# A hymba-style layer on one core: TensorE's order in the input stages written out by hand, with five queues of small steps behind the projection matmuls

## The chip, the core and the metric

The kernel runs on one core of a Trainium2 chip. A core has TensorE (PE in the profile, with its weight loads as PEld), VectorE (DVE), ScalarE (ACT), GpSimd (POOL), SyncE (SP, which issues the DMAs here) and 16 DMA engines. The metric is the device time of one execution in microseconds. Of the kernel before, three timed runs gave 1741.38 to 1743.57 us, with a median of 1742.06 us.

## The reference, cut to what matters

One transformer layer is applied to a prompt of 1024 tokens and to a sample sequence of 64 tokens (with a cache of 256 past frames and a recurrent state). All arrays are float32.

```python
def _layer(x, c, shift_prev, s_prev, k_past, v_past, logf_past, ...):
    mod = jax.nn.silu(c) @ w_ada + b_ada
    sh1, sc1, gt1, sh2, sc2, gt2 = jnp.split(mod, 6, axis=-1)
    h = _rms_norm(x, norm1_g) * (1 + sc1[:, None]) + sh1[:, None]
    proj = h @ w_in
    p_rwkv, p_fox = proj[..., :RWKV_COLS], proj[..., RWKV_COLS:]
    prev = jnp.concatenate([shift_prev, p_rwkv[:, :-1]], axis=1)
    z = p_rwkv + (prev - p_rwkv) * shift_mu
    r, k, v, dw, da, dg = jnp.split(z, list(RWKV_SPLITS), axis=-1)
    w_log = -jax.nn.softplus(-(w0 + jnp.tanh(dw) @ w_decay_up)) - 0.5
    decay = jnp.exp(-jnp.exp(w_log))
    a = jax.nn.sigmoid(a0 + da @ w_aaa_up)
    g = jax.nn.sigmoid(dg) @ w_gate_up
    kk = _heads(k * k_k, RWKV_HEADS)
    kk = kk / jnp.maximum(jnp.linalg.norm(kk, axis=-1, keepdims=True), 1e-12)
    k = k * (1 + (a - 1) * k_a)
    y, s_new = _rwkv_scan(r, decay, k, v, kk, a, s_prev)   # per token: S = S*w + (S.-kk)(kk*a)' + v k'
    y = group_norm(y) * gn_g + gn_b
    y_rwkv = (y + bonus(r, k, r_k, v)) * g
    q, kf, vf, fl = jnp.split(p_fox, list(FOX_SPLITS), axis=-1)
    q, kf = _rms_norm(q, fox_q_g), _rms_norm(kf, fox_k_g)
    logf = jax.nn.log_sigmoid(fl + fox_f_b)
    y_fox = _fox_mixer(q, k_all, v_all, cumsum(logf_all), past)   # causal softmax with a decay bias
    x = x + gt1[:, None] * (jnp.concatenate([y_rwkv, y_fox], axis=-1) @ w_out)
    h2 = _rms_norm(x, norm2_g) * (1 + sc2[:, None]) + sh2[:, None]
    x = x + gt2[:, None] * ((silu(h2 @ w_ffn_gate) * (h2 @ w_ffn_up)) @ w_ffn_down)
    return x, s_new, ...
```

The width is 1024, there are 8 rwkv heads and 8 attention ("fox") heads of 64, and the inner width of the last block is 2816.

## The kernel before, in words

Activations lie transposed, features on partitions. The tokens come in two halves (`Half`): the first has 512 tokens of the prompt and is one chunk of 512 columns; the second has the other 512 and the 64 sample tokens, in two chunks of 288. A float32 product is made of three fp32r matmuls, high by high, high by low and low by high, so that a projection column (128 outputs) takes 8 x 3 matmuls for each chunk (`mm3`, L294 to L296, tile `pmm`).

The kernel runs through a start (modulation, first norm), the input stage of the first half, that of the second half, the attention of both halves with the output product between, and the gated block with its down product. The change touches the two input stages alone, that is `phase` and what it calls. Each has 26 projection columns: two for the low-rank inputs (12 and 13), three for each of four pairs of rwkv heads (letter Z, in `proj_z`), and four each of Q, K and V for the attention. "Head" below stands for such a pair of rwkv heads. Around the columns stand these pieces, each with matmuls that are small:

- D, `rwkv_d` (L388): decay and learning rate of a head, from a low-rank product.
- A, `rwkv_a` (L417): key norm (`bsum`, L375), the chunk matrices pA (L464, 64*128 shapes), their masked copy `At`, a trip of 16x16 blocks through DRAM, and a solve of 31 small operations on VectorE (L485 to L491).
- B, `rwkv_b` (L500): the rest of the inversion in five groups of 32x32 matmuls (L523 and L549), transposes (L567, L575), and the state chain. It goes chunk by chunk (8 in the first half, 9 in the second): pR (L597), its copy R by VectorE and ScalarE (L599, L600), pSA (L610), its negated copy sv (L611, L612), pS (L613), and the new state (L617), with two pY beside it.
- N, `rwkv_n` (L628): group norm and gate of a head. L, `logf`: forget gates. q and k, `fox_norm` (L763): the norm of a Q or K column. C, `cache_kv`: cached keys and values. S, `x_stat1`: the norm of the second half's input. The modulation steps of the later stages (`ada_mm`, `ada_fin`) come from a list called `background`, one in front of each column.

`ORDER` gives the order in which these pieces are traced, as whole pieces, by letter and head. The order in which the engines run them is not this one. The framework's scheduler keeps a list of instructions for each engine, and picks by place in the trace and by its own estimate of when operands are ready, so that a later projection matmul may go ahead of an earlier small one. The order that it picks is then fixed in the program, and each engine runs its own in order. In the second half, the state chain of the last head (its B and N, `late`) is traced behind the input stage, and overlaps with the first half's attention.

PSUM has 8 banks: two for `mm` (projection, modulation, forget gates, statistics), two for `ra`, one for `fx`, one for `rb`, two for `ch`. Weights come through a ring of four raw tiles `wraw` (also used for modulation and for statistics), and are split into high (ScalarE, L212) and low (VectorE, L216). SP issues all DMAs.

Of the kernel before, what the change touches and what calls it, by code (L numbers as in the profile page):

```python
# [7 lines left out]
F32 = mybir.dt.float32  # L8
# [26 lines left out]
ORDER = ("Z0 D0 A0 L B0 D1 Z1 Q0 N0 A1 C0 Z2 q0 D2 V0 O A2 K0 k0 B1 K1 Z3 Q1 q1 V1 N1 D3 A3 V2 C1 S k1 Q2 Q3 B2 q2 N2 K2 k2 V3 K3 k3 C2 C3 q3",  # L35
         "T3 Z0 D0 A0 L Z1 K0 D1 U3 B0 A1 D2 Z2 Q0 N0 k0 A2 q0 D3 Q1 B1 K1 q1 Z3 A3 k1 V2 N1 V1 B2 V0 Q2 q2 K3 N2 Q3 q3 P B3 K2 k3 k2 V3")
# [28 lines left out]
class K:  # L65
# [115 lines left out]
    def ada_mm(self, t, raw=None, ptag="mm"):  # L181

        nc = self.nc
        if raw is None:
            raw = self.ada_load(t)
        ps = self.ps([P, 2, P], tag=ptag, name="pada")
        for s in range(2):
            for i in range(4):
                k = 2 * i + s
                last = nc.tensor.matmul(ps[32 * i:32 * i + 32, 0], self.ct[:, k], raw[:, k], start=(s == 0),  # L190
                                        stop=(s == 1))
        row = self.slot([P, P], name="mrow", tag="mrow")
        return t, ps, row, last, nc.scalar.copy(row, ps[:, 0])

    def ada_fin(self, part):
        nc = self.nc
        t, ps, row = part[:3]
        self.last = nc.tensor.transpose(ps[:, 1], row, self.ident)
# [33 lines left out]
    def x_stat1(self):  # L232

        nc = self.nc
        acc = self.zpool.tile([P, 576], F32, tag="z", name="xacc")
# [12 lines left out]
        return self.x_rms(Half(1), acc)  # L248

    def x_rms(self, hf, rs):  # L250
        nc, n = self.nc, hf.n
        for off, m in hf.chunks:
            ps = self.ps([P, 512], tag="mm", name="pxs")
            nc.tensor.matmul(ps[:, 0:m], self.ones, rs[:, off:off + m], start=True, stop=True)
            nc.scalar.activation(rs[:, off:off + m], ps[:, 0:m], AF.Ln, scale=1.0 / D, bias=self.eps_n)
# [53 lines left out]

    def proj_z(self, hf, zi):  # L310
# [8 lines left out]
        z = self.zpool.tile([P, 576], F32, tag="z", name="z")  # L319
# [44 lines left out]
    def lora(self, hf, j, w, rows, x, evac, tag):  # L364
        nc = self.nc
        for off, n in hf.chunks:
            ps = self.ps([P, 512], tag=tag, name="plora")
            nc.tensor.matmul(ps[:, 0:n], w[rows, j * P:(j + 1) * P], x[rows, off:off + n], start=True, stop=True)
            evac(ps[:, 0:n], off, n)

    def bsum(self, hf, w, x, evac, tag):
        nc = self.nc
        for off, n in hf.chunks:
            ps = self.ps([P, 512], tag=tag, name="pbs")
            nc.tensor.matmul(ps[:, 0:n], w, x[:, off:off + n], start=True, stop=True)  # L375
# [12 lines left out]
    def rwkv_d(self, hf, j, zl):  # L388
# [6 lines left out]
        for off, m in hf.chunks:  # L395

            ps = [self.ps([P, 512], tag="ra", name="plora") for _ in range(2)]
            for x in range(2):
                nc.tensor.matmul(ps[x][:, 0:m], self.whi2[x][:, j * P:(j + 1) * P], zl[:, x, off:off + m], start=True,
                                 stop=False)  # L400
            for x in range(2):
                nc.tensor.matmul(ps[x][:, 0:m], self.wlo2[x][:, j * P:(j + 1) * P], zl[:, x, off:off + m], start=False,
                                 stop=True)
            for x, (dst, base) in enumerate(((sw, V_W0), (a, V_A0))):
                nc.vector.tensor_scalar(dst[:, off:off + m], ps[x][:, 0:m], col(base), -43.0, op0=ALU.add, op1=ALU.max)
        self.sigm(sw[:, 0:n], 1.0)
        self.sigm(a[:, 0:n], 1.0)
        cum = self.slot(name="cum", tag="sa")
# [6 lines left out]
        return a, cum  # L415

    def rwkv_a(self, hf, j, z, d):  # L417

        nc, vc, O = self.nc, self.vc, self.O
# [4 lines left out]
        zk, zr, zv, sq = z  # L424
        a, ip = d
        pp = self.pp
# [5 lines left out]
            rn[:, off:off + m], ps, 1e-24, None, op0=ALU.max), "ra")  # L432
        nc.scalar.activation(rn[:, 0:n], rn[:, 0:n], AF.Ln, scale=1.0 / 64)
        nc.scalar.activation(rn[:, 0:n], rn[:, 0:n], AF.Exp, scale=-0.5)
        kk = self.slot(name="kk", tag="sa")
        nc.vector.scalar_tensor_tensor(kk[:, 0:n], zk[:, 0:n], self.kk8[:, j:j + 1], rn[:, 0:n], op0=ALU.mult, op1=ALU.mult)
        rk = self.rpool.tile([P, 9, P], F32, tag="rk", name="rk")
        kb = self.rpool.tile([P, 9, P], F32, tag="kb", name="kb")
        nc.vector.tensor_tensor(rk[:, 0:nch, 0:64], ch(kk), pp[:, 0:nch, 0:64], op=ALU.mult)
        nc.vector.tensor_tensor(rk[:, 0:nch, 64:128], ch(zr), pp[:, 0:nch, 1:65], op=ALU.mult)  # L440
        nc.vector.tensor_tensor(kk[:, 0:n], kk[:, 0:n], a[:, 0:n], op=ALU.mult)
        for h in range(2):
            hp = slice(64 * h, 64 * h + 64)
            nc.vector.tensor_tensor(kb[hp, 0:nch, hp], ch(kk)[hp], ch(ip)[hp], op=ALU.mult)
        nc.vector.tensor_scalar(a[:, 0:n], a[:, 0:n], col(V_KA), self.oka[:, j:j + 1], op0=ALU.mult, op1=ALU.add)
        nc.vector.tensor_tensor(zk[:, 0:n], zk[:, 0:n], a[:, 0:n], op=ALU.mult)
        for h in range(2):
            hp, oc = slice(64 * h, 64 * h + 64), slice(64 - 64 * h, 128 - 64 * h)
            nc.vector.tensor_tensor(kb[hp, 0:nch, oc], ch(zk)[hp], ch(ip)[hp], op=ALU.mult)

        nc.vector.scalar_tensor_tensor(zr[:, 0:n], zr[:, 0:n], col(V_RK), zk[:, 0:n], op0=ALU.mult, op1=ALU.mult)
        bon = self.slot(name="bon", tag="bon")
        self.bsum(hf, self.bones, zr, lambda ps, off, m: nc.vector.tensor_tensor(
            bon[:, off:off + m], ps, zv[:, off:off + m], op=ALU.mult), "ra")

        At = self.rpool.tile([P, 9, 2, 2, 64], F32, tag="At", name="At")
        for c in range(0, nch, 4):
# [3 lines left out]
            for i in range(m):  # L461
                for h in range(2):
                    hp = slice(64 * h, 64 * h + 64)
                    nc.tensor.matmul(pa[h][:, i], kb[hp, c + i], rk[hp, c + i], start=True, stop=True)  # L464
            for h in range(2):
                nc.vector.tensor_tensor(At[:, c:c + m, :, h], pa[h][:, 0:m].rearrange("p i (x t) -> p i x t", x=2),
                                        self.amask[:, h:h + 1].rearrange("p o (x t) -> p o x t", x=2)
                                        .to_broadcast([P, m, 2, 64]), op=ALU.mult)

# [9 lines left out]
        nc.sync.dma_start(mb[0:2 * nb], dm.rearrange("i g x s t -> (i g x) s t"))  # L479
        wb = self.rpool.tile([72, 16, 16], F32, tag="wb", name="wb")  # L480
# [4 lines left out]
        for s in range(15):  # L485
# [4 lines left out]
            nc.vector.tensor_tensor(wb[0:2 * nb, s + 1:16, 0:s + 1], wb[0:2 * nb, s + 1:16, 0:s + 1], t_, op=ALU.add)  # L490
        nc.vector.tensor_copy(mb[0:2 * nb], wb[0:2 * nb].rearrange("p s t -> p t s"))  # L491
# [6 lines left out]
        return zv, rk, kb, pc, bon, At, dw, du  # L498

    def rwkv_b(self, hf, j, st):  # L500

        zv, rk, kb, pc, bon, At, dw, du = st
        nc, vc, O = self.nc, self.vc, self.O
        n, nch = hf.n, hf.nch
        ng = 2 * nch
        col = lambda base: vc[:, base + j:base + j + 1]

# [7 lines left out]

        def small(name, blocks, mm):

            pg = [self.ps([P, 9, 32], tag=t, name=name) for t in ("rb", "ch")]
            for c in range(nch):
                for x in blocks:  # L520
                    for h in range(2):
                        r = slice(64 * h + 32 * x, 64 * h + 32 * x + 32)
                        nc.tensor.matmul(pg[h][r, c], *mm(h, c, r, slice(32 * x, 32 * x + 32)), start=True, stop=True)  # L523
# [4 lines left out]
        for h in range(2):  # L528
            hs = slice(64 * h, 64 * h + 64)
            nc.vector.tensor_tensor(g1[hs, 0:nch], pg[h][hs, 0:nch],  # L530
                                    self.qmask[hs].unsqueeze(1).to_broadcast([64, nch, 32]), op=ALU.mult)
        pg = small("pw1", (0,), lambda h, c, r, o: (inv[r, c, r], g1[r, c]))
        for h in range(2):
            r = slice(64 * h, 64 * h + 32)
            nc.vector.tensor_tensor(gt[r, 0:nch, 0:16], gt[r, 0:nch, 0:16], pg[h][r, 0:nch, 0:16], op=ALU.add)
        pg = small("pu1", (0, 1), lambda h, c, r, o: (g1[r, c], inv[r, c, r]))
# [1165 lines left out]
```

## Time and profile before

| | us |
|---|---|
| timed runs, median (lowest to highest) | 1742.06 (1741.38 to 1743.57) |
| the profiled execution, its own time | 1735.94 |
| its span, first to last instruction | 1734.2 |
| PE busy in the span | 1663.8 |
| VectorE busy | 1126.6 |
| ScalarE busy | 729.1 |
| first column of the first half's input stage starts | 35.0 |
| first column of the second half's starts | 329.8 |
| last projection matmul of the second half starts | 692.2 |

A row of a group reads: line, engine, operation, out<-in by the program's names, shape, count | busy us, mean ns of one | idle time of the engine before it, and what ended most of it. A row of a stretch reads: the stretch, its length, then the busy us (and instruction count) of PE, PEld, DVE, ACT and POOL, then the clock granted to TensorE as a share of the full one, the mean busy share of the DMA engines, and GB/s. A row of the timeline reads: start, duration, engine, line, operation, out<-in, shape, count. A float32 matmul that is not of the fp32r kind shows as two records. The ends of matmuls are modelled, so that the distance from one start to the next tells more than the duration. A row of waits reads: engine and line, the engine and line that released it, us in total, times, longest.

### The profile page before, as it was taken

To read this page: it belongs to the slowest core of one execution; us is meant where nothing else is said; L and a number is where in the kernel's file an instruction comes from. 1 tells how busy PE (TensorE), PEld (TensorE's weight loads), DVE (VectorE), ACT (ScalarE), POOL (GpSimd) and SP (SyncE) were. 2 spreads that over 40 slices of the span, in tenths; PEclk is the share of its full clock that TensorE was granted. 3 is DMA by queue.
4 is the path that set the end of the run, shared out by engine and by line. 5 is a ranking of instruction groups with operands and counts; after the bars stand their busy time and mean duration, and the time that the engine had idled before them with its cause. 6 is when DMAs were issued, how large, how long until landed. Compare 5 with 4: busy or idle time off the path is not lost.

```text
span 1734.2 us, 33257 instructions
## 1 busy us (share of the span) xinstructions
PE 1663.8 (96%) x12893; PEld 1447.9 (83%) x12893; DVE 1126.6 (65%) x2574; ACT 729.1 (42%) x1532; POOL 180.8 (10%) x412
## 2 busy tenths in 40 slices
PE   5999999999999999889999989999999999999999
PEld 3676766688888888766888889999999999999998
DVE  6676676757686753876877686666666655555545
ACT  4534454553454445765776453333233223211210
POOL 2102121131221212300210000000000000000000
PEclk9999999999899999989999999999999999999999
DMA  8535457632233344566553333222222224433213
GB/s 314 149 95 137 142 140 207 175 93 56 55 76 75 95 121 136 157 194 177 151 177 136 127 115 101 75 75 75 76 75 82 78 87 143 161 98 98 95 37 122
DMA packets 133581, 207.09 MB, mean 119 GB/s; under 512 B 62126, under 2 KB 70350, under 8 KB 133422
## 3 DMA queue, kind: packets, MB, share of 16 engines
q1 hardware_dynamic: 133422, 204.95, 39.3%
q8 instruction: 102, 1.67, 0.4%
q14 instruction: 57, 0.47, 0.1%
HBM read 157.65 MB, written 47.25 MB: 118 GB/s over the span
## 4 chain that ended last, share of the span: by engine, by line
PE 82%; DVE 7%; ACT 7%; DMA 2%; issue 2%; SPq 1%; POOL 0%; DVEq 0%; ACTq 0%; POOLq 0%
PE pd L1264 15%; PE pfc L1153 8%; PE pfe L1153 8%; PE pfa L1153 7%; PE pmm L294 5%; PE pmm L296 5%; PE pmm L295 5%; PE pfb L1153 4%; PE pav L962 2%; PE pbs L375 2%; PE pA L464 2%; PE ppt L940 2%; PE po L294 1%; PE po L295 1%; PE po L296 1%
## 5 line engine op out<-in xcount | busy, mean ns | idle before, releaser
L294 PE MATMUL pmm<-hhi,whi 128*128 128x288 f32 (+1 forms) x624 | 220.7, 354 | 0.7 <-ACT pb L317 0.7
L295 PE MATMUL pmm<-hlo,whi 128*128 128x288 f32 (+1 forms) x624 | 218.2, 350 | 0.0
L296 PE MATMUL pmm<-hhi,wlo 128*128 128x288 f32 (+1 forms) x624 | 218.0, 349 | 0.0
L212 ACT CAST whi<-wraw 128x1024 fp32r<-128x1024 f32 (+2 forms) x116 | 99.3, 856 | 214.4 <-PE pd L1264 167.0
L1264 PE MATMUL pd<-ah,wlo 128*128 128x512 f32 (+1 forms) x528 | 173.5, 329 | 0.0
L1264 PE MATMUL pd<-al,whi 128*128 128x512 f32 (+1 forms) x528 | 173.2, 328 | 0.0
L1264 PE MATMUL pd<-ah,whi 128*128 128x512 f32 (+1 forms) x528 | 173.0, 328 | 0.0
L1268 DVE SCALAR_TENSOR_TENSOR x1t<-pd,mod,x1t 128x512 f32<-128x512 f32 x192 | 91.4, 498 | 110.6 <-PE pd L1264 110.0
L294 PEld LDWEIGHTS pmm<-hhi,whi 128*128 128x128 f32 x624 | 120.3, 193 | 13.5 <-ACT pb L317 2.0
L296 PEld LDWEIGHTS pmm<-hhi,wlo 128*128 128x128 f32 x624 | 120.3, 193 | 10.9 <-issue 1.7
L295 PEld LDWEIGHTS pmm<-hlo,whi 128*128 128x128 f32 x624 | 120.4, 193 | 9.6 <-issue 0.7
L216 DVE TENSOR_TENSOR wlo<-wraw,whi 128x1024 fp32r<-128x1024 f32 (+2 forms) x108 | 103.8, 961 | 26.0 <-ACT whi L212 25.6
L1153 PE MATMUL pfc<-hh,hS 128*128 128x256 f32 (+1 forms) x352 | 102.0, 290 | 4.4 <-ACT hh L1055 4.4
L1264 PEld LDWEIGHTS pd<-al,whi 128*128 128x128 f32 x528 | 99.4, 188 | 7.7
L1264 PEld LDWEIGHTS pd<-ah,whi 128*128 128x128 f32 x528 | 99.3, 188 | 7.7
L1264 PEld LDWEIGHTS pd<-ah,wlo 128*128 128x128 f32 x528 | 99.2, 188 | 7.4
L1153 PE MATMUL pfc<-hl,hS 128*128 128x256 f32 (+1 forms) x352 | 102.3, 290 | 0.0
L1153 PE MATMUL pfc<-hh,lS 128*128 128x256 f32 (+1 forms) x352 | 102.0, 290 | 0.0
L1153 PE MATMUL pfa<-hl,whi 128*128 128x256 f32 (+1 forms) x352 | 101.8, 289 | 0.0
L1153 PE MATMUL pfa<-hh,whi 128*128 128x256 f32 (+1 forms) x352 | 101.7, 289 | 0.0
L1153 PE MATMUL pfa<-hh,wlo 128*128 128x256 f32 (+1 forms) x352 | 101.4, 289 | 0.0
L604 POOL TENSOR_SCALAR sd<-sv,pc 64x64 f32<-64x64 f32 x136 | 72.0, 529 | 172.9 <-DVE sv L617 156.6
(360 smaller groups left out, 4402.0 us busy)
## 6 DMA issues: line engine op xcount, KB each, us to landing
wraw<-in_w_in_dram SPq DMA_DIRECT2D x52, 512.0 KB
wada<-in_w_ada_dram SPq DMA_DIRECT2D x48, 512.0 KB
as<-actscr SPq DMA_DIRECT2D x22, 544.0 KB
wraw<-in_w_gate_dram SPq DMA_DIRECT2D x22, 512.0 KB
wraw<-in_w_up_dram SPq DMA_DIRECT2D x22, 512.0 KB
wraw<-in_w_down_dram SPq DMA_DIRECT2D x40, 256.0 KB
wraw<-in_w_out_dram SPq DMA_DIRECT2D x16, 512.0 KB
actscr<-sg SPq DMA_DIRECT2D x22, 288.0 KB
```

Of the source, the lines that this page charges most:

```text
L212: nc.scalar.copy(hi, src)
L216: eng.tensor_tensor(lo, src, hi.bitcast(F32), op=ALU.subtract)
L294: nc.tensor.matmul(ps[0:M, 0:n], whi[:, k, 0:M], xhi[:, k, off:off + n], start=(k == 0), stop=False)
L295: nc.tensor.matmul(ps[0:M, 0:n], whi[:, k, 0:M], xlo[:, k, off:off + n], start=False, stop=False)
L296: nc.tensor.matmul(ps[0:M, 0:n], wlo[:, k, 0:M], xhi[:, k, off:off + n], start=False, stop=(k == kt - 1))
L375: nc.tensor.matmul(ps[:, 0:n], w, x[:, off:off + n], start=True, stop=True)
L464: nc.tensor.matmul(pa[h][:, i], kb[hp, c + i], rk[hp, c + i], start=True, stop=True)
L604: nc.gpsimd.tensor_scalar(sd[hsl[h]], sv[hsl[h], c, h], pc[hsl[h], c], None, op0=ALU.mult)
L940: nc.tensor.transpose(pt[0:rows, b - b0, t * P:t * P + qn], p[0:qn, pc:pc + rows], self.ident[0:qn, 0:qn])
L1153: nc.tensor.matmul(ps, l[:, k], r[:, s, k], start=(first and k == 0 and y == 0), stop=(k == 3 and y == 2), skip_group_check=True)
L1264: nc.tensor.matmul(ps[:, 0:n], w[:, i], x[:, t:t + n], start=(i == 0 and y == 0), stop=(i == len(fs) - 1 and y == 2))
L1268: nc.vector.scalar_tensor_tensor(dst, ps[:, so - off:so - off + l], self.mod[:, 40 + o, b:b + 1], dst, op0=ALU.mult, op1=ALU.add)
```

## The change

All matmuls and transposes of the two input stages, from the column after the low-rank ones on, are pinned in the order in which they are traced: `self.te` is a wrapper, `Ordered`, that ties each PE instruction to the one traced before it. Other engines and the DMA queue are left to the scheduler, and so is PE in all other stages.

The pieces become generators, which give way between their steps. Five queues (`Jobs`) hold them: B the state chains, X the pieces D and A, Y the inversions (now a piece of their own, `rwkv_m`), F modulation, forget gates, fox norms, values and cache, and G norms and statistics. After every three projection matmuls `proj` calls `tick`, which takes one step from some of the queues: in the first half from B, X, Y and, in turn, F or G; in the second half in turn from B and X or from Y, F and G. `pause` lets a number of ticks pass, `drain` steps the queues with no projection between until a condition holds.

Other edits come with it. The raw weights are asked for two columns ahead, by a `plan` (`next_raw`), and split in the column before. `ORDER` is shorter, since B, N, q and k are now queued by their producers. P, which loads the first attention operands, waits until the last head's solve has been traced. The last head's chain and norm end in the input stage, and `late` is gone. `ch` has one bank in place of two, a new `yb` has one (the inversion and the transposes; both halves of a group share it), modulation and forget gates move from `mm` to `fx`, norms from `rb` to `ra`, and the slots `sb` are three in place of two.

```diff
-ORDER = ("Z0 D0 A0 L B0 D1 Z1 Q0 N0 A1 C0 Z2 q0 D2 V0 O A2 K0 k0 B1 K1 Z3 Q1 q1 V1 N1 D3 A3 V2 C1 S k1 Q2 Q3 B2 q2 N2 K2 k2 V3 K3 k3 C2 C3 q3",
-         "T3 Z0 D0 A0 L Z1 K0 D1 U3 B0 A1 D2 Z2 Q0 N0 k0 A2 q0 D3 Q1 B1 K1 q1 Z3 A3 k1 V2 N1 V1 B2 V0 Q2 q2 K3 N2 Q3 q3 P B3 K2 k3 k2 V3")
+ORDER = ("L O D0 Z0 A0 D1 Z1 A1 Q0 C0 C1 D2 Z2 A2 K0 V0 C2 C3 D3 Z3 A3 Q1 K1 S V1 Q2 K2 V2 Q3 K3 V3",
+         "L D0 Z0 A0 D1 Z1 A1 D2 Z2 A2 K0 D3 Z3 A3 Q0 K1 Q1 V0 V1 Q2 P Q3 V2 K2 K3 V3")
...
+    def tick(self, hf):
+        self.ticks += 1
+        t = self.ticks
+        for x in (("BX", "YFG")[t % 2] if hf.smp else ("BXYF", "BXYG")[t % 2]):
+            self.jobs[x].step()
+    def pause(self, hf, n):
+        t = self.ticks + n * (2 if hf.smp else 1)
+        while self.ticks < t and not self.draining:
+            yield
+    def drain(self, cond, queues="BXYFG"):
+        self.draining = True
+        while not cond():
+            left = [self.jobs[x].step() for x in queues]
+            assert any(left)
+        self.draining = False
...
     def proj(self, hf, col, evac):
-        if self.pre:
-            whi, wlo = self.pre.pop(0)
-        else:
-            if self.background:
-                self.background.pop(0)()
-            whi, wlo = self.load_w(self.A["w_in"][col // P], [P, KT, P])
-        for off, n in hf.chunks:
+        whi, wlo = self.pre.pop(0)
+        for x, (off, n) in enumerate(hf.chunks):
             ps = self.ps([P, 512], tag="mm", name="pmm")
-            self.mm3(ps, whi, wlo, self.hhi, self.hlo, KT, off, n)
+            for k in range(KT):
+                for y, (w, a) in enumerate(((whi, self.hhi), (whi, self.hlo), (wlo, self.hhi))):
+                    nc = self.nc
+                    self.te.matmul(ps[:, 0:n], w[:, k], a[:, k, off:off + n], start=(k == 0 and y == 0),
+                                     stop=(k == KT - 1 and y == 2))
+                self.tick(hf)
+                if x == 0 and k == 1:
+                    if not self.pre and self.raws:
+                        self.pre.append(self.split_w(self.raws.pop(0), [P, KT, P]))
+                    if len(self.raws) < 2:
+                        self.next_raw()
+                    if self.background:
+                        self.jobs["F"].add(None, self.background.pop(0))
             evac(ps, off, n)
...
@@ rwkv_b, of one chunk
             pr = self.ps([P, 2, 64], tag="ch", name="pR")
-            nc.tensor.matmul(pr, At[:, c, 0], sv[:, c], start=True, stop=True)
+            yield
+            self.te.matmul(pr, At[:, c, 0], sv[:, c], start=True, stop=True)
...
-            nc.tensor.matmul(py[:, c % 4], sv[:, c], rk[:, c], start=True, stop=False, skip_group_check=True)
+            self.te.matmul(py[:, c % 4], sv[:, c], rk[:, c], start=True, stop=False, skip_group_check=True)
+            yield
             pa = self.ps([P, 64], tag="ch", name="pSA")
-            nc.tensor.matmul(pa, inv[:, c], R, start=True, stop=True)
+            self.te.matmul(pa, inv[:, c], R, start=True, stop=True)
...
+            yield
+            self.te.matmul(pS, kbt[:, c], sv[:, c], start=True, stop=True)
...
@@ phase
             if op == "D":
-                d[j] = self.rwkv_d(hf, j, zl)
+                q["X"].add(None, self.rwkv_d(hf, j, zl))
             elif op == "Z":
...
             elif op == "A":
-                st[j] = self.rwkv_a(hf, j, z.pop(j), d.pop(j))
-            elif op == "B":
-                y[j] = self.rwkv_b(hf, j, st.pop(j))
+                q["X"].add(None, self.rwkv_a(hf, j))
+                q["Y"].add(None, self.rwkv_m(hf, j))
+                q["B"].add(None, self.rwkv_b(hf, j))
...
+        self.drain_f()
+        if hf.smp:
+            self.drain(lambda: not any(q.q for q in q.values()))
+        else:
+            self.drain(lambda: self.rs1 is not None)
...
+class Ordered:
+    def __init__(self, tc):
+        self.tc, self.e = tc, tc.nc.tensor
+    def matmul(self, *a, **k):
+        return self.tc.keep_in_program_order(self.e.matmul(*a, **k))
+    def transpose(self, *a, **k):
+        return self.tc.keep_in_program_order(self.e.transpose(*a, **k))
+class Jobs:
+    def __init__(self):
+        self.q, self.done = deque(), set()
+    def add(self, name, gen):
+        self.q.append((name, gen))
+    def step(self):
+        if not self.q:
+            return False
+        name, gen = self.q[0]
+        if next(gen, self) is self:
+            self.q.popleft()
+            self.done.add(name)
+        return True
```

More of the change, by code (lines that the diff above doesn't have):

```diff
@@ L1 @@
 import math
+from collections import deque
 from contextlib import ExitStack
@@ L189, in ada_mm @@
                 k = 2 * i + s
-                last = nc.tensor.matmul(ps[32 * i:32 * i + 32, 0], self.ct[:, k], raw[:, k], start=(s == 0),
+                last = self.te.matmul(ps[32 * i:32 * i + 32, 0], self.ct[:, k], raw[:, k], start=(s == 0),
                                         stop=(s == 1))
@@ L234, in x_stat1 @@
         nc = self.nc
-        acc = self.zpool.tile([P, 576], F32, tag="z", name="xacc")
+        yield from self.room(1)
+        acc = self.ztile("xacc")
         x = self.ring.tile([P, KT, 64], F32, tag="wraw", name="xs1")
@@ L367, in lora @@
             ps = self.ps([P, 512], tag=tag, name="plora")
[L368 removed]
+            self.te.matmul(ps[:, 0:n], w[rows, j * P:(j + 1) * P], x[rows, off:off + n], start=True, stop=True)
             evac(ps[:, 0:n], off, n)
@@ L449, in rwkv_a @@
             nc.vector.tensor_tensor(kb[hp, 0:nch, oc], ch(zk)[hp], ch(ip)[hp], op=ALU.mult)
+        yield
         nc.vector.scalar_tensor_tensor(zr[:, 0:n], zr[:, 0:n], col(V_RK), zk[:, 0:n], op0=ALU.mult, op1=ALU.mult)
+        yield
+        while 4 * hf.i + j - 2 not in self.ended:
+            yield
         bon = self.slot(name="bon", tag="bon")
@@ L497, in rwkv_a, with rwkv_m @@
                 nc.sync.dma_start(d[0:ng].rearrange("g x s t -> (g x) s t")[:, o, o], t[r])
[L498 to L506, printed above, removed]
+        self.solved[hf.i, j] = zv, rk, kb, pc, bon, At, dw, du
+    def rwkv_m(self, hf, j):
+        while (hf.i, j) not in self.solved:
+            yield
+        zv, rk, kb, pc, bon, At, dw, du = self.solved[hf.i, j]
+        nc, n, nch = self.nc, hf.n, hf.nch
         inv, gt = self.inv[j % 2], self.gt
@@ L1274, in down, with phase @@
             acts = new
-    def phase(self, hf, order, late):
+    def phase(self, hf, order):
         nc = self.nc
+        q = self.jobs
         with self.tc.issue_after(self.last.ins):
```

276 lines of the change are left out of this document (184 added, 92 removed).

## Prediction

> **What bounds the kernel now.** I read the page first, then the busy times of four stretches, then the granted clock of short stretches, then TensorE's waits, and last the timeline of single steps. The page:
>
> ```profile
> span 1734.2 us, 33257 instructions
> PE 1663.8 (96%) x12893; PEld 1447.9 (83%) x12893; DVE 1126.6 (65%) x2574; ACT 729.1 (42%) x1532; POOL 180.8 (10%) x412
> ```
>
> The profiled execution took 1735.94 us, 1.7 us of it outside the span; the timed median is 1742.06 us, 6.1 us more. I make the sum against the profiled execution and carry the difference over to the median. TensorE (PE) is the bound. The stretches, with each engine's busy time, the granted clock and DMA:
>
> ```profile
> 35.00:330.00 295.00, 284.78 (x2244) 204.38 (x2245) 205.04 (x544) 139.21 (x288) 51.32 (x120) 0.97 0.52 148
> 330.00:692.00 362.00, 352.14 (x3317) 299.68 (x3316) 236.91 (x641) 173.33 (x411) 78.65 (x161) 0.98 0.34 92
> 692.00:765.00 73.00, 62.10 (x381) 47.22 (x379) 60.11 (x195) 51.59 (x158) 17.05 (x55) 0.99 0.59 168
> ```
>
> The first two are the input stages of the two halves, the only stages whose order is edited; the third is the attention of the first half, mixed with what is left of head 3. PE idles 10.2 and 9.9 us in the input stages, 20.1 us of 657. So little is to be had from idle time as the profile counts it. Two losses hide in busy time: a halved clock, and a matmul that starts late while its predecessor's modelled end still runs. The clock:
>
> ```profile
> 142.00:149.00 7.00, 6.32 (x21) 4.31 (x22) 5.15 (x21) 6.03 (x12) 0.45 (x1) 0.52 0.81 228
> 285.00:295.00 10.00, 7.53 (x147) 5.09 (x146) 5.19 (x13) 6.91 (x15) 4.20 (x7) 0.69 0.77 181
> 455.00:470.00 15.00, 15.00 (x213) 12.76 (x214) 9.62 (x18) 4.20 (x11) 6.06 (x7) 0.66 0.13 37
> 535.00:545.00 10.00, 10.00 (x146) 8.80 (x145) 5.71 (x17) 6.43 (x13) 1.48 (x2) 0.66 0.08 14
> ```
>
> The missing shares of these four are 3.4 + 3.1 + 5.1 + 3.4 = 15.0 us.
>
> **The pace, and what a switch costs.** One triple of projection matmuls of the first half starts every 0.23 us, 0.70 in all; the rows around a group of pA:
>
> ```profile
> 118.27 0.40 PE L296 MATMUL pmm<-hhi,wlo 128*128 128x512 f32 x1
> 118.50 0.40 PE L294 MATMUL pmm<-hhi,whi 128*128 128x512 f32 x1
> 118.74 0.39 PE L295 MATMUL pmm<-hlo,whi 128*128 128x512 f32 x1
> 119.06 1.16 PE L464 MATMUL pA<-rk,kb 64*128 64x128 f32 x8
> 120.14 0.50 PE L296 MATMUL pmm<-hhi,wlo 128*128 128x512 f32 x1
> ```
>
> 118.74 to 119.06 is 0.32 us instead of 0.23: going to a 64*128 shape costs 0.09 us. In the second half a triple takes 0.40 us. One chunk of a head's state chain there, with the copies that it waits for (rows between left out):
>
> ```profile
> 366.85 0.46 PE L597 MATMUL pR<-sv,At 128*128 128x128 f32 x2
> ...
> 367.35 0.22 DVE L599 COPY R<-pR 64x64 f32<-64x64 f32 x1 [2.87 <-PE pR L597]
> 367.41 0.30 PE L296 MATMUL pmm<-hhi,wlo 128*128 128x288 f32 x1
> ...
> 367.81 0.29 PE L296 MATMUL pmm<-hhi,wlo 128*128 128x288 f32 x1
> 368.03 0.21 ACT L600 COPY R<-pR 64x64 f32<-64x64 f32 x1
> ...
> 368.11 0.46 PE L608 MATMUL pY<-rk,sv 128*128 128x128 f32 x2
> ...
> 368.40 0.33 PE L610 MATMUL pSA<-R,inv 128*128 128x64 f32 x2
> ...
> 369.05 0.21 DVE L611 TENSOR_SCALAR sv<-pSA 64x64 f32<-64x64 f32 x1
> ...
> 369.68 0.29 PE L296 MATMUL pmm<-hhi,wlo 128*128 128x288 f32 x1
> 369.70 0.22 ACT L612 ACTIVATE sv<-pSA 64x64 f32<-64x64 f32 x1
> ...
> 369.97 0.49 PE L613 MATMUL pS<-sv,kb 128*128 128x128 f32 x2
> ```
>
> 367.41 to 367.81 is the 0.40; one matmul is 0.13. Against that, pY starts 0.30 after the matmul ahead of it (0.17 late), pS 0.29 (0.16 late), pSA 0.07 late (0.29 after pY, whose two records take 0.22). That is 0.40 us a chunk, with idle time near nothing: this is the hidden loss, and in both cases the copy on ScalarE ends last (368.24 and 369.92), well after VectorE's.
>
> **The change part by part.** No arithmetic is added or removed. What changes is the order on PE, and the distance in it between a producer and its consumer: one triple (first half) or two (second half) plus whatever the other queues put between. Walked through by hand, the new order has 208 ticks in the first half and 416 in the second; 161 and 185 of them carry a small matmul step. No emptying of the queues meets a long backlog: the last chunk of the last head comes with the last projection column, so only one chunk and one norm stand after it, and (1,3) is solved just before P.
>
> *Clock.* Three of the four dips lie in or behind runs of 32x32 matmuls, with PE busy 15.00 of 15.00 us in one. The new order parts these runs by a triple or two, so I take those three away and keep one for the change of halves: 15.0 - 3.4 = 11.6, taken -11 (0 to -15). The Trainium skill, "TensorE: Matmul & The Clock Gate", "Why this matters for your kernels", asks for no idle gap over about 3 us between bursts; the dip at 455 to 470 has no idle time at all, so here the trace differs. By that rule taken alone the dips would not hang on what the change does, and the sum would be 11 us worse.
>
> *Shapes.* Counted along PE's timeline, the input stages have 140 visits to narrow shapes now, the first and the last being:
>
> ```profile
> 48.42 0.65 PE L190 MATMUL pada<-wada,ct 128*32 128x128 f32 x16
> ...
> 681.92 0.67 PE L549 MATMUL pu<-inv,gt 32*32 32x32 f32 x16
> ```
>
> The new order has about 93: 24 modulation steps, 20 groups of pA, 40 inversion steps, 9 of the forget gates. Each costs 0.09 us going in, and I take the same coming back: 47 x 0.18 = 8.5, taken -7 (0 to -9), since some visits follow each other. The Trainium skill, "TensorEngine Tiling (Array Packing)", "Key Properties", says that changing the tiling mode drains TensorE; the 0.09 us agrees. By that rule a step behind every triple would cost, were it not that today's order visits more often.
>
> *State chain.* 68 chunks x 0.40 = 27 us now. In the emptiest ticks of the new order pSA follows pR by some 1.1 to 1.2 us and pS follows pSA by 0.9 to 1.0 (own records plus 0.70, or 0.80 for two triples). The copies of the quoted chunk were ready 1.39 and 1.52 us after the start of pR and pSA on ScalarE, 0.72 and 0.86 on VectorE. So with ScalarE free there is no wait, with ScalarE as late as here 0.2 to 0.6 us a link in an empty tick and none in a full one. I take 0.34 a chunk, 23 us: -4 (+20 if ScalarE is always that late, -23 more if its copies follow at once).
>
> *Waits with a named releaser.* The largest are
>
> ```profile
> PE pbs L375 <- ACT fsq L759: 2.9, 3, 1.4
> PE plf L680 <- ACT fl L676: 1.9, 2, 1.5
> PE pu L549 <- ACT gt L545: 1.7, 2, 1.5
> ```
>
> Such pairs get at least a triple between them. Of the 20.1 us idle I take 8 away (0 to -11).
>
> *What the fixed order adds.* A waiting step now holds the next triple and all four other queues behind it. Where one step holds two matmuls for one bank, nothing can slip between: the two chunks of a fox norm in the second half share the single bank fx, and so do the two transposes of a value tile. Their evictions:
>
> ```profile
> L768 ACT ACTIVATE fsq<-pbs,eps_n 128x288 f32<-128x288 f32 x16 | 8.0, 500 | 4.6 <-PE pbs L375 4.5
> L816 ACT COPY tok<-pkv 128x512 f32<-128x512 f32 x3 | 1.8, 588 | 0.5 <-PE pkv L814 0.5
> ```
>
> Eight norms x (0.50 + 0.25) and four tiles x (0.59 + 0.25), where 0.25 is my estimate of start and handover from the chunk above: 6 + 3.4 = +9 (0 to +12). The inversion's five links a head are one step of queue Y apart, 40 links x 0.05 = +2 (0 to +8). At the change of halves hhi and hlo are rewritten, 16 + 16 VectorE operations:
>
> ```profile
> L272 DVE SCALAR_TENSOR_TENSOR hlo<-xk,mod,hhi x16: 278/512/753, 275.8 to 344.9; 128x64 fp32r<-128x64 f32 x8, 128x512 fp32r<-128x512 f32 x8
> L270 DVE SCALAR_TENSOR_TENSOR xk<-xk,g,xacc x16: 264/510/805, 272.8 to 339.4; 128x512 f32<-128x512 f32 x8, 128x64 f32<-128x64 f32 x8
> ```
>
> 32 x 0.51 = 16 us, against 6.4 us of the first column of the second half. Today a whole head's chain fills that; in the new order the chain of that head is done by then and only a norm is left: +3 (-3 to +8). DMAs move with their steps, all on SP's queue: weights are asked for two columns ahead, modulation tiles with their step, the inversion's small transfers between pauses of five triples. VectorE's one wait for the inversion's block was
>
> ```profile
> DVE tb L488 <- DMA mb<-dm: 2.0, 1, 2.0
> ```
>
> and a triple takes 0.70, so five triples and their steps cover it: 0.
>
> *Head 3 and the attention.* Today nine chunks and a norm of head 3 run inside the attention, whose VectorE is busy 60.11 of 73 us. In the new order they stand ahead of it: PE's work in the input stage grows by nine chunks at about 1 us (the records above) and 3 us of norm, +12, and VectorE is relieved of, among others,
>
> ```profile
> L617 DVE SCALAR_TENSOR_TENSOR sv<-pS,pc,sd 64x64 f32<-64x64 f32 x14 | 4.0, 283 | 2.0 <-PE pS L613 1.7
> ```
>
> in all some 12 us by such rows: 0 (-8 to +12).
>
> Sum: -11 - 7 - 4 - 8 + 9 + 2 + 3 + 0 = **-16 us**: 1720 for the profiled execution, 1726 for the median.
>
> **Rivals.** (a) *Slower.* The copies on ScalarE and VectorE sit behind long operations, and the fixed order makes each link pay. The point is 16 us over 68 x 3 = 204 links, 0.08 us a link beyond my 0.11. With 0.31 a link, 0.2 more, it is 204 x 0.2 = 41 - 16 = +25: 1767 us. For it: ScalarE ended 0.66 us after VectorE at pSA. Against it: a copy is now traced next to its matmul, not behind a whole head's work. Chance 0.25. (b) *No change.* The waits move from one place to the next, or the pinned order is nearly what PE does today (it already mixes projection and steps at 96% busy): 1742, 0.10. (c) *Much faster.* Copies follow at once and the chain's 23 us go too: -39, 1703, 0.15. (d) *The dips stay*, because light steps still fill the gate's measure: -5, 1737, 0.08; the page of the clock gate would side with this.
>
> **How the numbers follow.** The forecast has 0.42. Faster by over 0.2% (3.5 us, about what a measurement can tell from no change): 0.42 + 0.15 + 0.08 = 0.65; within it 0.10; slower 0.25. The range reaches to 1694, (c) with 9 us of its bounds, and to 1758, two thirds of the way into (a). The forecast's own range is 1705 to 1740.
>
> **What would show it.** Right: the last projection matmul ends before 690 us although head 3's chain has ended too; a clock of 1.00 through the inversion steps; at most 0.11 us of delay a link; the attention of the first half shorter than 73 us. Wrong: PE rows with pbs, pSA or pS after a copy on ScalarE adding up to more than 40 us; a first column of the second half over 20 us long; clock dips as many as now.

## The result, and the profile after

The changed kernel takes 1789.28 us (median of 4 runs, 1786.12 to 1795.38) against 1742.06 for the kernel before: ratio 1.0274, 95% interval 1.0239 to 1.0309. Medians and ratios of the kernel before are those of its fast runs throughout (one at 5358.38 us here and one at 3094.45 later are left out). The changed kernel is slower, and the forecast was 1726. The profiled execution took 1786.12 us, 50.2 more than the one before. The page, its first two lines:

```profile
span 1784.4 us, 33293 instructions
PE 1633.3 (92%) x12893; PEld 1425.8 (80%) x12893; DVE 1133.5 (64%) x2574; ACT 729.9 (41%) x1532; POOL 187.8 (11%) x412
```

As many matmuls as before, 30 us less of busy time in a span 50 us longer: TensorE waits. The input stages of the two halves, as stretches (length; PE, weight loads, DVE, ACT, POOL busy; granted clock; DMA share; GB/s):

```profile
38.90:375.00 336.10, 298.88 (x2574) 210.57 (x2574) 226.88 (x601) 158.63 (x340) 70.40 (x155) 0.95 0.46 137
375.00:737.00 362.00, 309.03 (x3062) 275.52 (x3059) 225.58 (x608) 159.30 (x376) 77.33 (x155) 0.96 0.31 85
```

The reader should see three things. The first half's stage is 41 us longer, the second as long as before (now with most of head 3's chain of its own half inside, and without that of the first). Part of the 41 us is work moved forward: the first stage runs 2574 matmuls where it ran 2244, the second 3062 for 3317. PE idles 37.2 + 53.0 = 90.2 us where it idled 20.1. And the granted clock fell, from 0.97 and 0.98 to 0.95 and 0.96, where the forecast had it rise. The 50.2 us lie as follows, by the first and last projection and the scores of the attention: 3.9 before the first projection (38.9 for 35.0), 40.3 in the first half, 1.0 between the halves, -0.6 in the second, 1.8 in the attention, 3.8 after it.

What PE waited for, by releaser (us in total, times, longest; view of the waits of PE). These are the pairs that the text uses; pada behind mrow (4.9), pR behind sv (3.9) and plora behind xl (3.6) are among those left out:

```profile
PE pbs L1740 <- DVE z L524: 11.3, 3, 7.2
PE pw L1740 <- issue: 10.3, 4, 4.7
PE pS L1740 <- ACT sv L712: 9.3, 13, 2.4
PE pbs L1740 <- ACT fsq L889: 7.8, 8, 1.3
PE pu L1740 <- DVE gt L642: 7.5, 5, 2.7
PE pvt L1743 <- ACT sv L617: 7.0, 4, 2.4
PE pg L1740 <- DMA gt<-dw: 2.7, 4, 0.8
PE pkvs L1743 <- ACT tok L950: 2.4, 3, 0.9
```

No pair of before had more than 2.9 us in these stages, and the bonus sum (pbs behind z) had waited once:

```profile
PE pbs L375 <- DVE z L451: 0.2, 1, 0.2
```

The longest wait shows how they come about (timeline; SCALAR_TENSOR_TENSOR and the like are VectorE's; rows between left out):

```profile
435.51 0.82 DVE L502 SCALAR_TENSOR_TENSOR kk<-z,kk,sq 128x576 f32<-128x576 f32 x1 [1.56 <-ACT sq L500]
436.36 0.76 DVE L509 TENSOR_TENSOR rk<-kk,pp 128x576 f32<-128x576 f32 x1
...
436.60 0.29 PE L1740 MATMUL pmm<-hhi,wlo 128*128 128x288 f32 x1
...
441.71 1.51 DVE L521 TENSOR_TENSOR kb<-z,cum 64x576 f32<-64x576 f32 x2
443.24 0.82 DVE L524 SCALAR_TENSOR_TENSOR z<-z,vc 128x576 f32<-128x576 f32 x1
...
444.11 2.29 PE L1740 MATMUL pbs<-z,bones 128*128 128x288 f32 x4 [7.22 <-DVE z L524]
445.79 0.85 PE L1740 MATMUL pmm<-hhi,whi 128*128 128x288 f32 x1
```

The steps from kk to the bonus sum are a few ticks of 0.4 us apart on PE, but hand VectorE 8.5 us of work without a break (435.51 to 444.06, with two operations of a projection column, L387 and L388, in between). PE is through its triples by 436.9 and then stands for 7.2 us in front of the bonus sum, with the next projection, whose data are there, behind it. The waits put down to "issue" ahead of pw are of the same kind: one of 4.73 us ends at 491.15, just after VectorE has written g (490.13 and 0.92 us long), which had stood behind six operations of that run.

Counted along PE's timeline from one matmul's start to the next, and sorted by what the two are, the input stages were and are:

```
                            before              after
projection to projection    291.7 us (1549)     305.8 us (1528)
projection to step           88.3    (323)      150.2    (344)
step to step                252.9   (3369)      214.5   (3416)
step to projection           24.8    (322)       27.7    (343)
```

So the change did what it was meant to inside the steps: 38 us less. It lost 62 us in front of them, and 14 between projections. Of these 14, some 5 are the half clock (53 of the pairs start in it, for 37 before, at about twice the usual distance), and some 5 are waits of pmm for a weight split or for hhi and hlo.

### The profile page after: what moved, and what is told of

Same layout as the page of the kernel before. It is cut to its first block, busy times and chain, and to the rows that moved or that the text cites. A ratio compares the mean times of both kernels' runs of the same rounds, so it can differ in the third digit from the quotient of the medians.

```text
span 1784.4 us, 33293 instructions
## 1 busy us (share of the span) xinstructions
PE 1633.3 (92%) x12893; PEld 1425.8 (80%) x12893; DVE 1133.5 (64%) x2574; ACT 729.9 (41%) x1532; POOL 187.8 (11%) x412
## 3 DMA queue, kind: packets, MB, share of 16 engines
q1 hardware_dynamic: 133422, 204.95, 37.4%
## 4 chain that ended last, share of the span: by engine, by line
PE 72%; DVE 10%; ACT 9%; issue 4%; DMA 3%; SPq 1%; POOL 0%; DVEq 0%; ACTq 0%; POOLq 0%
PE pd L1400 15%; PE pmm L1740 10%; PE pfe L1289 7%; PE pfc L1289 7%; PE pfa L1289 7%; PE pfb L1289 4%; PE pav L1098 2%; PE pbs L1740 2%; PE ppt L1076 2%; PE po L304 1%; PE po L306 1%; PE po L305 1%; DVE wlo L222 1%; ACT whi L218 1%; PE psc L1046 1%
## 5 line engine op out<-in xcount | busy, mean ns | idle before, releaser
L1740 PE MATMUL pmm<-hhi,whi 128*128 128x288 f32 (+1 forms) x608 | 244.3, 402 | 3.1 <-ACT whi L218 1.7
L1740 PE MATMUL pmm<-hlo,whi 128*128 128x288 f32 (+1 forms) x608 | 202.5, 333 | 1.1 <-DVE hlo L282 1.1
L1740 PE MATMUL pmm<-hhi,wlo 128*128 128x288 f32 (+1 forms) x608 | 201.9, 332 | 0.9 <-DVE wlo L222 0.9
```

What stands on the lines that cost most here:

```text
L1740: return self.tc.keep_in_program_order(self.e.matmul(*a, **k))
```

## The experiments

Each kernel below is the changed one with one edit, unless its text says more. They were run in four groups, each with its own runs of the kernel before: e_unpin, e_unpin1, e_space and e_banks (median of the kernel before 1743.24), e_pinS, e_pinP, e_small and e_best (1740.78), e_pool and e_pinSs (1742.47), e_nolo and e_light (1741.92).

**Without the pin (e_unpin).**

```diff
-        self.te = Ordered(self.tc)
+        self.te = nc.tensor
```

> The queues, the prefetch and the banks of the changed kernel are kept; only the pin goes, so TensorE's order is again the scheduler's choice. Theory A (distance): the fixed order sends TensorE into steps whose inputs still lie in VectorE's and ScalarE's queues; its named waits grew from 20 to 90 us in the input stages. Without the pin other matmuls go ahead of such a step: named waits at most 40 us, 1740 to 1760 us. Rival B (banks: ch and yb are single now): the waits are for a bank, no order avoids them, 1775 us or more. Rival C (the order in which the steps are written, pinned or not, is what costs): 1775 us or more too.

1737.88 us, ratio to before 0.9983 (0.9963 to 1.0003), 2 us under the lower end that theory A gave it. The stretches of its two stages, and its largest waits in them:

```profile
39.20:352.40 313.20, 300.45 (x2562) 212.38 (x2563) 220.37 (x594) 155.24 (x332) 68.82 (x155) 0.96 0.51 147
352.40:690.00 337.60, 322.88 (x3072) 279.16 (x3070) 224.33 (x614) 162.29 (x382) 78.05 (x154) 0.97 0.34 91
```

```profile
PE pkbt L605 <- DVE kb L521: 8.7, 1, 8.7
PE pY L707 <- POOL rk L667: 2.2, 4, 1.0
```

PE idles 12.8 + 14.7 = 27.5 us. The whole loss hangs on the pin: queues, prefetch and banks as changed cost nothing that can be measured without it. B and C fall as the cause of it. VectorE's run still costs something here: the 8.7 us (79.8 to 88.5) are PE standing behind the run of the first head, with half clock for 17.1 us from 84.8 on. The stages are 23 and 24 us shorter than with the pin, so each half gives back about the same.

**Pin in the first half only (e_unpin1).** The same line, with `nc.tensor if hf.smp else Ordered(self.tc)`.

> The pin is kept in the first half and taken away in the second, whose named waits are 53 us and whose clock dips cost 15 us. Theory A: the second half gives back most of the 28 us by which its delays outside the dips grew and half of the dips' 7, 1755 to 1768 us; the first half's stage stays at 335 us. Rivals B and C: 1780 us or more.

1765.02 us, ratio 1.013 (1.01 to 1.0161), as theory A had it. The second stage takes 334.0 us, the first 339.5 (4 more than expected).

**Which way the pin holds (e_pinS, e_pinP).** In e_pinS the projection's matmuls call `nc.tensor.matmul`, the steps stay Ordered; in e_pinP it is the reverse.

> Only the steps stay pinned, each behind the projection triple written before it; the projection matmuls are free and may go ahead of a step that isn't ready. Theory A (a step whose input is late holds the projection behind it): the projections fill the waits, 1738 to 1755 us, named waits of the input stages under 45 us. Theory A2 (what costs is that a step can't be taken earlier than its place): 1775 us or more.

> The reverse: the projection matmuls stay pinned behind whatever is written before them, the steps are free to go earlier or together. Theory A: the triple behind a late step still waits for it, 1775 to 1795 us. Theory A2: 1738 to 1755 us.

Steps pinned and projections free: 1741.92 us, 1.0006 (0.9987 to 1.0025). Projections pinned and steps free: 1771.38, 1.0168 (1.0142 to 1.0194), 4 us under the lower end that A gave it and 16 over A2's. The stages of e_pinS:

```profile
38.10:356.60 318.50, 294.34 (x2566) 208.37 (x2567) 220.88 (x595) 153.23 (x331) 73.47 (x155) 0.97 0.49 141
356.60:691.50 334.90, 319.71 (x3057) 275.53 (x3055) 225.09 (x610) 161.82 (x383) 76.23 (x151) 0.98 0.35 95
```

and of e_pinP:

```profile
38.80:379.50 340.70, 311.08 (x2571) 219.74 (x2571) 222.66 (x600) 158.94 (x338) 70.97 (x155) 0.92 0.47 134
379.50:723.00 343.50, 310.73 (x3062) 275.54 (x3062) 223.30 (x609) 159.62 (x378) 78.67 (x156) 0.97 0.33 90
```

Idle time is 39.4 us in the one and 62.4 in the other. That a step keeps its place costs little; that the next triple may not pass it costs most of the 47 us. Free projections take back all of it, free steps alone 18 us.

**More distance (e_space).** A `yield` after each VectorE operation of the run. The edit gives six more steps a head; its expectation counts five.

> The pin stays; only the distance grows: each VectorE operation of the part from kk to the bonus product gets a step of its own, five more steps a head on queue X, so that no step hands VectorE more than one long operation. Theory A: the waits behind that run (bonus sum 11.3 us, pw 10.3, pu on gt 7.5, part of pS on sv) fall by some 20 us, and a dip or two with them: 1760 to 1772 us. Rival B: no bank changes, 1786 to 1792. Rival C: the order is as before but for the longer gaps, 1785 or more.

1806.58 us, 1.0382 (1.0341 to 1.0423): a miss, and the other way. In the first half the stage did get 7 us shorter (329.3), though its idle time did not (39.0). In the second it took 390.0. Queue X became too long there, as I read the kernel, and the loops that empty the queues (for a free z slot, and at P) now ran chains with no projection between. Projection matmuls alone, in four such stretches (second number: PE busy, with its count):

```profile
501.60:508.60 7.00, 0.00 (x0) 0.05 (x1) 0.46 (x2) 0.66 0.27 76
552.50:560.30 7.80, 0.03 (x1) 0.10 (x1) 0.53 (x2) 0.66 0.03 6
578.20:586.30 8.10, 0.00 (x0) 0.05 (x1) 0.55 (x2) 0.75 0.08 9
677.40:689.80 12.40, 0.00 (x0) 0.03 (x1) 0.71 (x2) 0.79 0.37 96
```

35 us in all. Counted over both stages, stretches of 5 us or more without a projection are eight with 59 us, where the changed kernel has three with 20. Half clock went from 57.8 us to 91.9, which alone is 17 us more lost, as much as the kernel is slower. Distance in a fixed order is paid in queue length, and there was no room for it.

**The banks (e_banks).** ch gets two banks, yb shares those of ra, the start uses ch and ra.

> The pin stays; ch has two banks again as in the kernel before, and what used yb shares the two banks of ra; the modulation tiles at the start use ch and ra as before. Theory A: only the start (3.9 us later than before) and the second value transpose of the odd chunk (7.0 us) come back, 1777 to 1783 us; the other waits stay. Rival B: the single banks are the cause, 1765 us or less.

1791.62 us, 1.0297 (1.0259 to 1.0334): no gain. The start came back (first projection at 34.9), and then the first half took as much longer (339.6 for 336.1, the second 367.5 for 362.0). A's sum falls, and rival B gets no support. The edit is not a clean test of B, since it also puts the inversion and the transposes on the two banks of ra: the 7.0 us of pvt behind sv are gone, and 6.8 us of a new pair stand in their place,

```profile
PE pkbt L1743 <- DVE sw L461: 6.8, 5, 2.7
```

behind an operation that empties a bank of ra.

**Two small bank waits (e_small).** `("yb", "ch")[t // 2 % 2]` at the start; a `yield` between the two chunks of a fox norm.

> Pinned as in the changed kernel, with two single banks relieved: the modulation tiles of the start go to ra, yb, ra, ch in turn, and the two chunks of a fox norm stand a step apart. Start: the first projection some 4 us earlier (35 in place of 38.9). Fox norm: of 7.8 us of waits behind its own eviction at most 2 are left. Together 1777 to 1783 us; if these waits are only handed on to the next late step, 1786 to 1790 us.

1782.01 us, 1.0238 (1.0208 to 1.0267): 7 us, as expected where the waits are not handed on, though this interval overlaps that of the changed kernel. The first projection starts at 35.8, and no wait behind fsq is left in the list.

**The start's banks without the pin (e_best), both bank edits with pinned steps (e_pinSs).**

> No pin, and the start's tiles in ra, yb, ra, ch. Theory A: as without the pin (1738), less up to 4 us of the start: 1733 to 1738 us, 0.2 to 0.5 per cent under the kernel before. If the start's delay is taken up by a later wait: 1738 to 1742 us.

> Steps pinned, projections free (1742), with the two small bank edits (start's tiles in ra, yb, ra, ch; the fox norm's chunks a step apart), which gave 7 us under the full pin. Theory A: a free projection already fills the fox norm's wait, so only the start's 3 to 4 us are left: 1736 to 1740 us. If both add up as under the pin: 1733 to 1736.

1740.10 us, 0.9991 (0.9973 to 1.0008), and 1742.37, 1.0005 (0.999 to 1.002). Neither gains on its parent: the first projection is 4.3 and 2.8 us earlier, and the medians don't show it. For e_best that is the second case of its expectation, for e_pinSs a miss of both. No version here beats the kernel before by more than can be measured.

**Work off VectorE: by GpSimd (e_pool), or left out (e_nolo).** In e_pool the weights' low parts are made with `pool_lo=True` in the input stages; in e_nolo `split_w` returns the high part twice there.

> Pinned as in the changed kernel; the second part of each weight split (wlo, 51 operations of 1.22 us on VectorE in the input stages, 62 us) goes to GpSimd, where the trace has such operations at 2.38 us. If the steps are late because VectorE's queue is long (theory A's cause of the lateness), 62 us less of it take 15 to 30 us off the named waits: 1760 to 1778 us. If they are late for the length of their own chain, or wait for ScalarE, or if the state product on GpSimd now comes late in VectorE's place: 1784 us or more.

> Pinned as in the changed kernel. Left out: the low part of the projection weights; the third matmul of a triple reads the high part once more, so TensorE's work is the same, and VectorE is rid of 51 operations of 1.22 us (62 us of its 452 in the input stages) with nothing added on GpSimd. If the steps are late because of VectorE's backlog: 15 to 30 us off, 1760 to 1775 us. If they are late for the length of their own chain or for ScalarE: 1783 us or more.

e_pool took 1839.55 us, 1.0559 (1.054 to 1.0578). It says nothing on theory A, since VectorE's busy time did not fall (460 us in the stages, for 452): its operations grew as GpSimd's ran. One pair in its timeline:

```profile
440.10 2.37 POOL L222 TENSOR_TENSOR wlo<-wraw,whi 128x1024 fp32r<-128x1024 f32 x1 [3.54 <-ACT whi L218]
440.24 2.67 DVE L387 TENSOR_SCALAR z<-pb,omu 128x512 f32<-128x512 f32 x2 [0.28 <-ACT pb L372]
```

e_nolo puts the question without GpSimd: 1777.41 us, 1.0202 (1.0179 to 1.0225), 12 us under the changed kernel, between the two expectations. The edit takes away 49 of the 51 operations; VectorE's busy time in the stages falls by 52 us (452 to 400). That much less work, spread over the stages, takes a quarter of the loss.

**The run itself, shorter (e_light).**

```diff
-        nc.vector.tensor_tensor(kk[:, 0:n], kk[:, 0:n], a[:, 0:n], op=ALU.mult)
-        for h in range(2):
...
-            nc.vector.tensor_tensor(kb[hp, 0:nch, hp], ch(kk)[hp], ch(ip)[hp], op=ALU.mult)
+        nc.vector.scalar_tensor_tensor(kb[:, 0:nch, 0:64], ch(kk), 0.01, ch(ip), op0=ALU.mult, op1=ALU.mult)
...
```

> Pinned as in the changed kernel. Left out: in the run from kk to the bonus product, the two products with a, its scaling, and one of the two halves of each write of kb (the values are wrong); the run falls from 8.3 to 4.7 us a head, 29 us of VectorE in all, and its place in the order stays. If this run is what the bonus sum, pw and pu wait behind: their 29 us of named waits fall by half, and 1768 to 1778 us. If another operation takes its place: 1783 us or more.

1767.25 us, 1.0151 (1.0123 to 1.0179): 22 us less, 1 us under the lower end of the expectation, with 29 us of VectorE's busy time left out where e_nolo leaves out 52. The bonus sum's wait is gone from the list altogether, and

```profile
PE pw L1733 <- issue: 3.8, 3, 2.1
PE pu L1733 <- DVE gt L635: 5.1, 4, 2.3
```

stand where 10.3 and 7.5 stood: 29.1 us became 8.9. Intervals at half clock that begin inside the stages fell from 57.8 us to 37.4. So what counts most is not how much VectorE has to do, but that one stretch of it lies between two steps that stand close together on PE.

## Why the prediction was wrong

The step that failed is "Such pairs get at least a triple between them. Of the 20.1 us idle I take 8 away (0 to -11)". For the three pairs that it names it held: their 6.5 us became 0.5. It failed for pairs that had hardly waited before. A triple is 0.40 or 0.70 us; what lies on VectorE between the step with kk and the bonus sum is up to 8.5 us, because X hands over a whole head's products in a few steps. Idle time went from 20.1 to 90.2 us, +70 where -8 stood. The prediction had seen that "a waiting step now holds the next triple and all four other queues behind it", but priced it only for the copies of the chain, where two matmuls share one bank, in the inversion and at the change of halves. The hold behind VectorE's long run it put at nothing. e_unpin, e_pinS and e_pinP show that this hold is the loss, e_light that a run shorter by some 3.6 us a head (29 us over eight heads) takes back close to half of it (22 of 47 us). What makes the rest was not taken apart; the list names ScalarE's copies in the chain, the second value transpose behind its own bank, and the fox norm.

Point by point, with the measured value (the terms overlap; idle time holds several of them):

- *Clock*, -11: wrong in sign. Intervals at half clock that begin in the stages went from 4 (30.6 us) to 12 (57.8 us), 14 us more lost. I took light matmul runs for the cause, and did not see that new waits would open new dips. Of the four intervals before, two follow 3.4 us with PE busy throughout, behind 32x32 matmuls as I had it; dips of this kind did go. After, of eleven idle gaps of 2 us or more, nine are followed by half clock within 2 us, and in three of these it begins while PE is still waiting, as in these two:

```profile
441.40:448.20 6.80, 4.09 (x14) 3.24 (x16) 4.97 (x9) 0.00 (x0) 0.30 (x2) 0.50 0.23 71
489.20:496.00 6.80, 4.85 (x118) 4.47 (x119) 5.67 (x12) 2.11 (x6) 1.39 (x2) 0.50 0.01 2
```

  The other three of the twelve follow 3.4 us in which several shorter waits add up:

```profile
130.80:134.20 3.40, 1.90 (x13) 1.13 (x11) 2.84 (x4) 1.50 (x3) 0.00 (x0) 1.00 0.41 66
260.60:264.00 3.40, 2.01 (x61) 1.32 (x63) 3.31 (x7) 0.00 (x0) 0.00 (x0) 0.99 0.45 154
625.80:629.20 3.40, 1.86 (x45) 1.61 (x44) 3.32 (x7) 1.24 (x3) 0.00 (x0) 1.00 0.79 261
```

  The clock changes here in steps of 3.41 us. Of the changed kernel's full-clock steps, the nine with PE busy for 1.08 us or less were all followed by half clock; of nine with 1.68 to 2.03 us three were; above that none was. The Trainium skill, "TensorE: Matmul & The Clock Gate", "Why this matters for your kernels", asks for no idle gap over about 3 us. I had set it aside for a dip without a gap; here the four gaps over 3 us agree with it, and of the seven of 2 to 3 us five did it too (237.2 and 609.2, of 2.4 us, are two; one of 2.4 at 474.5 did not).
- *Shapes*, -7: right. Entries from 128*128 matmuls into narrower shapes went from 132 to 98 (the prediction counts 140 and has 93), 34 x 0.18 = 6.1. The 0.09 us of the way back, which the prediction only assumed, is there too: behind 32*32 matmuls the next projection starts 0.12 us after the last, behind most small 128*128 ones 0.03.
- *State chain*, -4: late starts of pR, pY, pSA and pS, against the usual distance behind the same kind of matmul, are 29 to 33 us in the stages before and 28 to 36 after, as one takes the usual distance. That is 0.14 to 0.18 us a link for the 0.11 taken, and the sign of the term stays open. Rival (a) decided at 0.19.
- *Single bank fx*, +9: 7.8 behind fsq and 2.4 ahead of pkvs, 10.2. Right; e_small took the waits behind fsq away, though only some 4 of its 7 us can be theirs, since 3 are the start's.
- *Inversion*, +2 (0 to +8): pw 10.3 and pu 7.5, together 17.8. Wrong by the same cause: g and gt stood in VectorE's queue behind the run. The transfers, for which "five triples and their steps cover it: 0" stood, left PE 2.7 us (pg behind gt), and VectorE waited 6.4 us for the block mb where it had waited 2.0.
- *Change of halves*, +3: the first column of the second half took 11.0 us in place of 16.7, so about -6, 3 us past the lower bound.
- *Head 3 and the attention*, 0: the attention took 1.8 us longer. The number lies in the range, but the relief behind it, some 12 us, did not show, though eight of head 3's nine chunks had left the attention. The last chunk and the norm still stand at its head (740.05 to 752.71 on PE), where the change meant them to end before it, and the attention has 30.7 us at half clock for 20.5.
- Not in the sum: the start. The modulation tiles use yb, now one bank, in place of the two of ch; the first projection is 3.9 us later, and e_banks and e_small bring it back. The 3.8 us after the attention lie nearly all in the gated block, which has 13.7 us at half clock for 6.8; what caused that was not looked into.

Rival (a) had the sign, with a chance of 0.25, but put it in the chain's links, at 1767. Its counterargument, that a copy now stands next to its matmul and "not behind a whole head's work", is what 435.51 to 444.11 refutes: only PE was fixed, and VectorE still got the head's work in one piece. Of the prediction's three signs of being wrong only the clock dips came. Its 40 us were to stand behind copies on ScalarE, which came to 23; the longest waits stood behind VectorE, for which no sign was set.

## What to carry to other kernels

Before you fix an in-order engine's sequence, put beside each pair of producer and consumer the time that the producer's own queue needs between them, and not the number of instructions on the fixed engine; a step whose input is late costs what it holds up, and where idle time takes up two thirds of a clock step of 3.41 us, a stretch at half clock as well. If you must fix the small steps, leave the filler work free to pass them: that alone (e_pinS) took back the whole 47 us here. Distance bought with more steps lengthens the queue, and is only free where the queue has room.

## What the runs showed of the hardware

While GpSimd subtracted two SBUF tiles, VectorE's work from SBUF stood still, and its work from PSUM did not. In e_pool GpSimd's 128x1024 subtraction took 2.39 us a piece, and VectorE's scaling of a 128x512 tile went from

```profile
L387 DVE TENSOR_SCALAR z<-pb,omu 128x512 f32<-128x512 f32 x28 | 13.5, 482 | 4.5 <-ACT pb L372 4.5
```

in the changed kernel to

```profile
L387 DVE TENSOR_SCALAR z<-pb,omu 128x512 f32<-128x512 f32 x28 | 34.0, 1213 | 20.2 <-ACT pb L372 20.1
```

The row of VectorE in the pair shown above merges two operations. The first, of 128x512, took 2.51 us (440.24 to 442.75) in place of 0.48 and ended 0.28 us after GpSimd's: it stood until GpSimd was through. All twelve of this form that started during such a subtraction ended 0.28 us after it. Counted up to 792 us, of 37 operations of VectorE that read only SBUF and started during one (0.3 us or more before its end), 36 ended after it. Operations that read PSUM kept their pace: all 23 took their usual time within 0.01 us. One stretch shows both kinds, first from PSUM (plora), then from SBUF (pb):

```profile
189.83 2.39 POOL L222 TENSOR_TENSOR wlo<-wraw,whi 128x1024 fp32r<-128x1024 f32 x1 [2.37 <-PE plora L1740]
190.44 0.74 DVE L461 TENSOR_SCALAR a<-plora,vc 128x512 f32<-128x512 f32 x1
191.17 1.33 DVE L387 TENSOR_SCALAR z<-pb,omu 128x512 f32<-128x512 f32 x1
```

The Trainium skill, "Trainium Architecture — The Big Picture", "What this means for kernel authors", calls the port that these two share an exclusive lock; for the operations that read SBUF the trace agrees.
